# A list scheduler that models the memory port shared by VectorE and GpSimd and picks the engine by it

## The chip, the core and the metric

The kernel runs on one core of one Trainium2 chip. A core has TensorE (PE in the profile; its weight loads are shown apart as PEld), VectorE (DVE), ScalarE (ACT), GpSimd (POOL) and SyncE (SP, which here issues all loads and stores), with the memories SBUF and PSUM beside them. The metric is the time of one execution on the device in microseconds (us); runs are compared by their medians.

## The reference

Two networks of two layers each are applied one after the other to the same tensor of 512 tokens by 1024 features, in float32.

```
for l in 0, 1:                                  # first block
    p = rmsnorm(x) @ w_in                       # latents of q and kv, rotary key, a and gate
    attention of 8 heads over 512 tokens (latents up-projected, softmax, values)
    u = silu(layernorm(dwconv31(a * sigmoid(gate))))          # 31 taps over the tokens
    x = x + concat(attention, u) @ w_o
    z = dwconv3(rmsnorm(x) @ w_up);  x = x + (silu(zg) * zv) @ w_down   # 2816 wide
x = rmsnorm(x)
for l in 0, 1:                                  # second block
    m = state_space_mixer(x) if l == 0 else gated_linear_recurrence(x)
    x = layernorm(ALPHA * x + m)
    x = layernorm(ALPHA * x + relu(x @ w1)**2 @ w2)           # 4096 wide
    x = x + sigmoid(x @ w_gate) * (p[l] @ w_proj)
```

## The kernel before

The activations lie feature-major: eight tiles of 128 features by 512 tokens hold x for the whole run. Every product runs in float32r on operands that are split exactly into a high part and a low part, and takes three products (high with high, high with low, low with high) for each 128 x 128 block of a weight matrix (`mm3`, `dense`). The weights are not preloaded: SP loads them unit by unit, 512 KB each as a rule, into three buffers "r". For each unit `weights` (L662) makes the parts: a cast `hi` (by `copy`, L659, on ScalarE or VectorE) and a subtraction `lo = src - hi` (`R.either`, on GpSimd or VectorE), both 128 x 512. Activations are split in the same way by `split_from`.

The stages are, in order: mixer 0 (attention and convolution, `mixer1`, L856), feed-forward 0 (`ffn1`, L1049), mixer 1, feed-forward 1, the state space mixer (`ssd`, L1110), the first squared-relu feed-forward (`mlp`, L1461), the embedding gate (`ple`), the gated recurrence (`hgrn`, L1294), the second `mlp` and `ple`. In a mixer `conv_tile` (L956) runs once for every two heads: 17 of the 31 taps are a chain of multiply-adds on VectorE (an input tile "u" in SBUF, the running sum in SBUF); the other 14 are scaled on ScalarE and added by `R.either` operations. The softmax of a head works on its four query blocks, each with a minimum on VectorE, an exponential on ScalarE, a reciprocal, a scaling, four transposes on TensorE, a copy and a subtraction. `hgrn` treats its eight heads one after the other: a tree of decays built of many half-width operations on VectorE and GpSimd (`R.other`, `R.either`), then short products.

Nothing of this is issued as it is written. The program is recorded: `R.tensor`, `R.vector` and so on make an `Op` with its cost in a model of the core (`cost`, L340; `cost_tensor`, L366), the operations it depends on, and its tiles. An `R.either` operation may run on GpSimd (first choice) or VectorE, an `R.other` operation on VectorE (first choice) or GpSimd (L322); `any` (L380) gives an operation in several forms, the first of them the first choice, as `copy` does with ScalarE before VectorE. The model's costs in ns, for n columns: VectorE 69 + 1.041 n (copies and scalar operations without PSUM 69 + 0.52 n), plus 60 for each per-partition scalar; GpSimd 147 + 2.105 n; ScalarE 93 + 0.833 n, or 51 + 0.833 n where PSUM takes part; a product 2.5 + n / 2.4.

`schedule` (L441) then plays the core. At each step it asks every engine for its best ready operation by the key (earliest start, priority, place in the program), where the earliest start is the latest of the engine's own free time, the ends of the operations before it with a latency for each pair of engines (`LAT`, L323), and buffers; and it takes the best over the engines. The priority is place in the program, less 0.015 of the remaining path, plus 150 for a change of the activation table and plus `second` = 2000 when the engine is not the operation's first choice. An engine that isn't the first choice may take an operation only if it ends no later than the first choice would, plus `eager` = 500 ns. An operation that needs a new buffer must leave some for older operations that still wait for theirs: `KEEP` (L591), two of the eight PSUM banks among them. Operations up to 2400 places behind the oldest open one take part. The result is a fixed order for each engine; on the chip every queue is worked in this order, and semaphores enforce the dependences. All instructions are issued in `issue` and so bear its line (L572) in the profile.

The groups of the profile name tiles by class: "s" is SBUF of up to 2 KB to a partition, "r" raw weights, "u" padded convolution inputs, "t" and "n" small tiles, "V" and "C" vectors and constants.

Of the kernel before, what the change touches and what calls it, by code (L numbers as in the profile page):

```python
# [38 lines left out]
# ---------------------------------------------------------------- weight units  # L39
def weight_units():  # L40
    """(name, layer, first row, row tiles, column pieces); a piece is (start, stop) or (None, zeros)."""
    u = []
# [99 lines left out]
# ---------------------------------------------------------------- small vectors  # L142
def vec_layout():
    """name -> (first column, columns)"""
    o, n = {}, 0

    def add(name, k):
        nonlocal n
        o[name] = (n, k)
        n += k  # L150
    for l in range(DEPTH):
        for name, k in (("g_mix", 8), ("g_q", 3), ("g_kv", 2), ("w_dw_conv", 124), ("b_dw_conv", 4), ("g_conv_ln", 4),
                        ("b_conv_ln", 4), ("g_ffn", 8), ("w_dw_ffn", 132), ("b_dw_ffn", 44)):
            add(f"{name}{l}", k)
    for name, k in (("g_final", 8), ("cw", 96), ("cb", 24), ("nw", 16), ("dskip", 16), ("dtb", 32), ("alog", 32),
                    ("lb", 8), ("hnw", 1), ("ln_g", 32), ("ln_b", 32), ("rope", 6)):
        add(name, k)
    return o, n
# [50 lines left out]
def constants():  # L209
    """[128, *] of 0 and 1: identity, s<=l, all ones, rope sum, two-way selector, level masks"""  # L210
    i = np.arange(P)
    eye = (i[:, None] == i[None, :])
    tri = (i[:, None] <= i[None, :])
    add = np.zeros((P, P))
    for m in range(P):
        add[m % 32::32, m] = 1
    sel = np.zeros((P, 32))
    for k in range(64):
        sel[k, k % 32] = 1
    j, t = i[:, None], i[None, :]  # L220
    mk = []
    for h in LEVELS:
        mk.append((j // (2 * h) == t // (2 * h)) & (j % (2 * h) < h) & (t % (2 * h) >= h))
    return np.ascontiguousarray(np.concatenate([eye, tri, np.ones((P, P)), add, sel] + mk, axis=1).astype(np.float32))
# [5 lines left out]
# ---------------------------------------------------------------- recorded program and its schedule  # L230
class Tl:
    """A tile of the recorded program; its memory is chosen when the program is scheduled."""
# [11 lines left out]
class Ap:  # L244
    """An access pattern on a recorded tile: the steps to rebuild it and the elements it covers."""
# [68 lines left out]
class Op:  # L314
    __slots__ = ("i", "eng", "calls", "cost", "preds", "succs", "npred", "ready", "tiles", "start", "end", "prio", "label", "tab", "tail", "bias", "alts", "done")


class Recorder:
    """Takes the instructions in program order, orders them per engine by a simulation of the core, and issues them."""
# [8 lines left out]
    def __init__(self):  # L328
        self.ops, self.bias, self.label, self.switch = [], 0, "", 150
        self.greed, self.order_w, self.second, self.eager = 0.015, 1.0, 2000, 500  # L330
# [34 lines left out]

    def cost_tensor(self, calls):  # L366
        """A product streams its columns while the weights of the next one load."""
        stream, load = [], []
        for meth, args, kw in calls:
            n, m = args[0].n, args[1].n  # L370
            once = meth == "transpose" or args[1].tl.dt == F32R
            stream += [2.5 + n / 2.4] if once and meth != "transpose" else [2.5 + n / 1.2] * (1 if once else 2)
            load += [107 * m / 128] * (1 if once else 2)
        return sum(max(a, b) for a, b in zip(stream, load[1:] + [107]))

    def together(self, calls):
        """Products of the tensor engine that stay in one run."""
        self.add("tensor", "matmul", (), {}, [("matmul", a, k) for a, k in calls])

    def any(self, *forms):  # L380
        """One operation in several forms (engine, method, arguments, options); the schedule picks one."""
        eng, meth, args, kw = forms[0]
        self.add(eng, meth, args, kw)
        self.ops[-1].alts = [(e, self.cost(e, m, a, k), [(m, a, k)]) for e, m, a, k in forms]

    def add(self, eng, meth, args, kw, calls=None):
        o = Op()
        calls = calls or [(meth, args, kw)]
        if eng == "tensor":
            o.alts = [(eng, self.cost_tensor(calls), calls)]  # L390
        else:
            o.alts = [(e, self.cost(e, meth, args, kw), calls) for e in self.EITHER.get(eng, (eng,))]
        eng = o.alts[0][0]
# [47 lines left out]
    def schedule(self, slots, keep, window=2400):  # L441
        """Order all operations. slots: class -> buffers; keep: class -> buffers that an operation
        leaves for older operations that still have to take theirs."""
# [28 lines left out]
        table, loads = None, 0  # L472
        while n < len(ops):
# [3 lines left out]
            for p in self.PARTS:  # L477
                t0 = busy[p]
                cand = None
                for o in ready[p]:  # L480
# [5 lines left out]
                    s = max(t0, s)  # L486
# [26 lines left out]
                    if not ok:  # L513
                        continue
                    key = (s, o.prio + (self.switch if load else 0) + (self.second if p != o.alts[0][0] else 0), o.i)
# [6 lines left out]
            (s, _, _), o, p = best  # L522
            o.start = s
            o.eng, o.cost, o.calls = [x for x in o.alts if x[0] == p][0]
# [3 lines left out]
            if o.eng == "sync":  # L528
                size = o.tiles[0].shape[0] * int(np.prod(o.tiles[0].shape[1:])) * 4
                busy["sync"] = s + max(60, size / 330.0)  # L530
                o.end = s + 2000 + size / 330.0
            else:
                o.end = s + o.cost
                if o.tab and table not in o.tab:
                    table = o.tab[0]
                    o.end += 1283
                    loads += 1
                busy[o.eng] = o.end
            n += 1
# [35 lines left out]
# activation tables: function -> the sets that hold it; a set stays loaded while it serves  # L575
# [13 lines left out]
# ---------------------------------------------------------------- the program  # L589
SLOTS = {"psum": 8, "r": 3, "s": 86, "u": 4, "t": 12, "n": 24, "V": 1, "C": 1}  # L590
KEEP = {"psum": 2, "s": 18, "u": 2, "t": 6, "n": 16}  # L591
# [7 lines left out]
def record(R, xT, pos, wts, vecs, consts, pT, outT, dbg=None, stop=None):  # L599
# [37 lines left out]
    def stacked(name, l):  # L637
        """The next unit, of at most 64 columns, with its two float32r parts side by side."""
# [23 lines left out]
    def weights(name, l=None):  # L662
        """The next unit: loaded, and split exactly into two float32r parts."""
# [25 lines left out]
    # ------------------------------------------------ helpers  # L689
# [56 lines left out]
    def gained(name):  # L746
        """x * g as an operand; the row factor is applied to the products"""
        op = []
# [45 lines left out]
    def project(name, l, a, cuts=FULL, scale=None, then=None):  # L794
        """x += a @ w for the row tiles in a, over units of 256 columns"""
# [12 lines left out]
    def products(name, l, n, op, use, cuts=FULL, cols=P):  # L808
        """use(i, slice, product) for n units against op"""
# [9 lines left out]
    # ------------------------------------------------ rope tables  # L819
# [35 lines left out]
    # ------------------------------------------------ block 1: attention and convolution mixer  # L855
    def mixer1(l):  # L856
# [55 lines left out]
        # shared rotary key, four copies down the partitions  # L912
# [16 lines left out]
        # row factors of the latents on all partitions  # L929
# [7 lines left out]
        # values, token-major  # L937
# [39 lines left out]
        for h in range(HEADS):  # L977
# [45 lines left out]
            # the parts of v lie in the two halves of the rows  # L1023
# [12 lines left out]
        # norm and gate of the convolution branch  # L1036
# [11 lines left out]
    # ------------------------------------------------ block 1: gated feed-forward  # L1048
# [60 lines left out]
    # ------------------------------------------------ block 2, layer 0: state space mixer  # L1109
    def ssd(op):  # L1110
# [3 lines left out]
        # step sizes, token-major  # L1114
# [13 lines left out]
        # log(1 + e) = 2 atanh(e / (2 + e)), e = exp(-|x|)  # L1128
# [164 lines left out]
    # ------------------------------------------------ block 2, layer 1: gated linear recurrence mixer  # L1293
    def hgrn(op):  # L1294
# [11 lines left out]
        # lower bound: softmax over the layers, running sum, less the first  # L1306
# [10 lines left out]
        for h in range(8):  # L1317
            # log forget gate and input gate
# [32 lines left out]
            # running sums of the log gates over 64 tokens, then the decay tree below them  # L1351
# [30 lines left out]
            # over a whole chunk: decay from its start and to its end  # L1382
# [9 lines left out]
            # scores [s, l] of the four chunks  # L1392
# [19 lines left out]
            # states between the chunks  # L1412
# [19 lines left out]
            # normed by token, then back to features  # L1432
# [27 lines left out]
    # ------------------------------------------------ block 2: squared relu feed-forward  # L1460
# [24 lines left out]
    # ------------------------------------------------ block 2: per-layer embedding gate  # L1485
    embedded = {}

    def embed(l, half):
        """Half of p @ w_proj. It waits for nothing else: it can stand where the tensor engine would idle."""
# [50 lines left out]
    # ------------------------------------------------ the two blocks  # L1540
    R.label = "start"
    # products of zeros while the first loads run: they open the clock gate of the tensor engine
# [88 lines left out]
```

## Time and profile before

| | |
|---|---|
| time of the runs | 2942.33, 2937.53, 2938.12 us; median 2938.12 |
| the profiled execution: span from the first to the last instruction | 2940.1 us; its own time is not listed apart, and the span stands for it |
| instructions | 37496 |
| mean granted TensorE clock | 0.977 |
| DMA | 235.26 MB, mean 80 GB/s |
| GpSimd's instructions | 1163 |
| VectorE's instructions | 2962 |
| ScalarE's instructions | 2162 |

A group of instructions is shown as: line, engine, operation, what it writes <- what it reads (by class of tile), shapes, x count | busy us, mean ns of one | idle time of the engine just before them, and what ended it. The duration of one instruction counts from where the engine begins on it, so that a wait inside the instruction (for a memory port, say) shows as a longer instruction and not as idle time. Busy time is the union of the instructions; consecutive ones overlap a little in the records, so sums of durations come out somewhat above it.

### The profile page before, as it was taken

The page shows a single profiled execution, that of the slowest core. Times are in us where ns is not written, and L with a number is a line of the kernel's source. Part 1 is how long each engine was busy: PE and PEld are TensorE (multiplying, and loading weights), DVE is VectorE, ACT ScalarE, POOL GpSimd, SP SyncE. Part 2 cuts the span into 40 slices and gives each one's busy share as a digit, 9 for nine tenths or more (in the row PEclk, how much of TensorE's full clock was granted, in tenths as well). Part 3 has the DMA queues.
Part 4 walks back from the last instruction along what each step waited for, and adds up shares of the span by engine and source line. Part 5 has one row for each costly group of instructions (what it writes and reads, how often), then busy time and mean ns, then how long its engine had stood idle before and what let it go on. Part 6 is the DMA issues. An engine that isn't in the chain of part 4 may idle for free. (4 is left out here: it accounts for less than half of the span.)

```text
span 2940.1 us, 37496 instructions
## 1 busy us (share of the span) xinstructions
PE 2778.7 (95%) x14054; PEld 2283.6 (78%) x14054; DVE 2051.8 (70%) x2962; ACT 1193.5 (41%) x2162; POOL 1459.2 (50%) x1163
## 2 busy tenths in 40 slices
PE   7788999999788999999999999999989999899999
PEld 5566788888577888887667888888878788788888
DVE  8999777766998766675674665455687777745546
ACT  4585332335584332244553333122345563322223
POOL 5786434454875334462254563344564544434443
PEclk8899999999899999999999999999999999999999
DMA  4003213331013223331112422233231113223230
GB/s 161 13 24 122 72 65 108 115 126 35 9 58 115 72 100 94 102 108 37 37 44 79 124 70 95 92 106 109 64 94 44 51 51 99 75 93 108 94 108 30
DMA packets 69445, 235.26 MB, mean 80 GB/s; under 512 B 7824, under 2 KB 11024, under 8 KB 69264
## 3 DMA queue, kind: packets, MB, share of 16 engines
q1 hardware_dynamic: 69264, 232.87, 24.7%
q8 instruction: 111, 1.82, 0.2%
q14 instruction: 70, 0.57, 0.1%
HBM read 230.74 MB, written 2.10 MB: 79 GB/s over the span
## 5 line engine op out<-in xcount | busy, mean ns | idle before, releaser
L572 PE MATMUL psum<-s,s 128*128 128x512 f32 (+2 forms) x12752 | 2709.8, 370 | 73.1 <-DVE s L572 49.7
L572 PEld LDWEIGHTS psum<-s,s 128*128 128x128 f32 (+1 forms) x12752 | 2167.4, 190 | 521.8 <-DVE s L572 62.5
L572 POOL TENSOR_TENSOR s<-r,s 128x512 fp32r<-128x512 f32 (+1 forms) x632 | 894.1, 1434 | 903.6 <-ACT s L572 452.0
L572 POOL TENSOR_TENSOR s<-s,s 128x512 f32<-128x512 f32 (+4 forms) x395 | 468.3, 1201 | 379.0 <-DVE s L572 215.5
L572 ACT CAST s<-r 128x512 fp32r<-128x512 f32 (+1 forms) x681 | 385.4, 609 | 381.8 <-DMA r<-wts 340.1
L572 DVE TENSOR_TENSOR s<-s,s 128x512 fp32r<-128x512 f32 (+4 forms) x453 | 418.3, 935 | 84.9 <-ACT s L572 70.1
L572 DVE TENSOR_TENSOR s<-s,psum 128x512 f32<-128x512 f32 (+2 forms) x400 | 224.6, 590 | 284.0 <-PE psum L572 283.2
L572 DVE SCALAR_TENSOR_TENSOR s<-u,V,s 128x512 f32<-128x512 f32 x304 | 324.1, 1076 | 52.5 <-ACT s L572 49.1
L572 ACT ACTIVATE s<-s 128x512 f32<-128x512 f32 (+1 forms) x338 | 188.8, 578 | 281.5 <-DVE s L572 279.5
L572 ACT ACTIVATE s<-psum 128x512 f32<-128x512 f32 (+2 forms) x174 | 91.5, 527 | 453.3 <-PE psum L572 449.1
L572 ACT ACTIVATE s<-u,V 128x512 f32<-128x512 f32 x200 | 144.3, 760 | 258.2 <-DVE u L572 257.8
L572 DVE TENSOR_TENSOR s<-r,s 128x512 fp32r<-128x512 f32 (+1 forms) x237 | 235.7, 1010 | 12.9 <-ACT s L572 9.3
L572 PE MATMUL psum<-C,s 128*128 128x128 f32 (+1 forms) x500 | 93.2, 282 | 53.2 <-POOL s L572 26.4
L572 DVE SCALAR_TENSOR_TENSOR s<-psum,s 128x512 f32<-128x512 f32 (+1 forms) x88 | 55.7, 638 | 112.1 <-ACT s L572 112.1
L572 DVE CAST s<-r 128x512 fp32r<-128x512 f32 (+1 forms) x188 | 101.3, 554 | 42.3 <-DMA r<-wts 42.2
L572 PEld LDWEIGHTS psum<-C,s 128*128 128x128 f32 x500 | 66.3, 157 | 73.0 <-POOL s L572 27.9
L572 DVE CAST s<-s 128x512 fp32r<-128x512 f32 (+1 forms) x105 | 105.8, 1008 | 8.1 <-POOL s L572 2.9
L572 DVE TENSOR_TENSOR u<-psum,s 128x512 f32<-128x512 f32 x88 | 60.5, 687 | 71.1 <-PE psum L572 70.7
L572 ACT CAST s<-s 128x512 fp32r<-128x512 f32 (+2 forms) x110 | 63.4, 587 | 99.8 <-DVE s L572 86.8
L572 ACT ACT_TABLE_LOAD x70 | 89.8, 1283 | 17.7 <-DVE s L572 14.2
L572 DVE SCALAR_TENSOR_TENSOR s<-psum,V,s 128x511 f32<-128x511 f32 (+4 forms) x90 | 66.4, 745 | 38.7 <-ACT s L572 32.9
L572 DVE TENSOR_TENSOR s<-psum,s 128x512 fp32r<-128x512 f32 (+3 forms) x131 | 84.8, 678 | 3.8 <-PE psum L572 2.1
(85 smaller groups left out, 1052.7 us busy)
## 6 DMA issues: line engine op xcount, KB each, us to landing
r<-wts SPq DMA_DIRECT2D x415, 512.0 KB, 3.6
r<-wts SPq DMA_DIRECT2D x12, 256.0 KB, 2.7
r<-wts SPq DMA_DIRECT2D x8, 384.0 KB, 3.0
s<-xT SPq DMA_DIRECT2D x8, 256.0 KB, 5.8
s<-pT SPq DMA_DIRECT2D x8, 256.0 KB, 4.0
outT<-s SPq DMA_DIRECT2D x16, 128.0 KB, 1.7
r<-wts SPq DMA_DIRECT2D x9, 128.0 KB, 2.1
V<-vecs SPq DMA_DIRECT2D x1, 480.5 KB, 6.7
```

Of the source, the lines that this page charges most:

```text
L572: getattr(eng, meth)(*[res(a) for a in args], **{k: res(v) for k, v in kw.items()})
```

## The change

The scheduler's model and its rules are changed; the recorded program, its operations and their forms stay.

- `shares` says of an operation on an engine whether it uses the shared port: on GpSimd always; on VectorE when it has more than one input of more than one column outside PSUM, and for `tensor_scalar` and `tensor_copy` when the input and the output both lie outside PSUM.
- `schedule` keeps a time `port`, the end of the last operation that uses the port. An operation that shares it can't start before that time, so two of them never overlap in the plan.
- `drag`: in the key, the start of an operation on an engine is set back by half of what it costs there above its cheapest engine. The plan itself uses the true start.
- `second` goes from 2000 to 0 and `eager` from 500 to 0.
- A product of n columns costs 2.5 + n / 2.28 ns in the model instead of 2.5 + n / 2.4.
- `KEEP` holds four PSUM banks for older operations instead of two.

Comments and docstrings are removed too; those lines are left out here.

```diff
@@ class Op
-    __slots__ = ("i", "eng", "calls", "cost", "preds", "succs", "npred", "ready", "tiles", "start", "end", "prio", "label", "tab", "tail", "bias", "alts", "done")
+    __slots__ = ("i", "eng", "calls", "cost", "preds", "succs", "npred", "ready", "tiles", "start", "end", "prio", "label", "tab", "tail", "bias", "alts", "done", "shared")
@@ class Recorder
-        self.greed, self.order_w, self.second, self.eager = 0.015, 1.0, 2000, 500
+        self.greed, self.order_w, self.second, self.eager, self.drag = 0.015, 1.0, 0, 0, 0.5
...
+    @staticmethod
+    def shares(eng, meth, args, kw):
+
+        if eng != "vector":
+            return eng == "gpsimd"
+        out = kw["out"] if "out" in kw else args[0]
+        ins = list(args if "out" in kw else args[1:]) + [v for n, v in kw.items() if n not in ("out", "accum_out")]
+        near = sum(isinstance(a, Ap) and a.n > 1 and a.tl.cls != "psum" for a in ins)
+        if meth in ("tensor_scalar", "tensor_copy"):
+            return near == 1 and out.tl.cls != "psum"
+        return near > 1
+
...
-            stream += [2.5 + n / 2.4] if once and meth != "transpose" else [2.5 + n / 1.2] * (1 if once else 2)
+            stream += [2.5 + n / 2.28] if once and meth != "transpose" else [2.5 + n / 1.2] * (1 if once else 2)
...
     def any(self, *forms):
...
+        self.ops[-1].shared = {e: self.shares(e, m, a, k) for e, m, a, k in forms}
...
     def add(self, eng, meth, args, kw, calls=None):
...
+        o.shared = {e: eng != "tensor" and self.shares(e, meth, args, kw) for e, _, _ in o.alts}
...
     def schedule(self, slots, keep, window=2400):
...
-        table, loads = None, 0
+        table, loads, port = None, 0, 0.0
...
-                    s = max(t0, s)
+                    s = max(t0, s, port) if o.shared[p] else max(t0, s)
...
                     if not ok:
                         continue
+                    s += self.drag * ([x[1] for x in o.alts if x[0] == p][0] - min(x[1] for x in o.alts))
                     key = (s, o.prio + (self.switch if load else 0) + (self.second if p != o.alts[0][0] else 0), o.i)
...
             (s, _, _), o, p = best
+            o.eng, o.cost, o.calls = [x for x in o.alts if x[0] == p][0]
+            s -= self.drag * (o.cost - min(x[1] for x in o.alts))
             o.start = s
-            o.eng, o.cost, o.calls = [x for x in o.alts if x[0] == p][0]
...
                 busy[o.eng] = o.end
+                if o.shared[p]:
+                    port = o.end
...
-KEEP = {"psum": 2, "s": 18, "u": 2, "t": 6, "n": 16}
+KEEP = {"psum": 4, "s": 18, "u": 2, "t": 6, "n": 16}
```

## The prediction

> **What bounds the kernel now.** I read the page first, then the busy time of each engine by stage, then the groups of instructions of each stage with their shapes kept apart, and last the waits and single stretches of the timeline.
>
> ```profile
> span 2940.1 us, 37496 instructions
> ...
> PE 2778.7 (95%) x14054; PEld 2283.6 (78%) x14054; DVE 2051.8 (70%) x2962; ACT 1193.5 (41%) x2162; POOL 1459.2 (50%) x1163
> ```
>
> TensorE stands idle for 2940.1 - 2778.7 = 161 us. Busy times by stage, from the view that cuts the span at the times I give it (columns: stretch, length, then PE, PEld, DVE, ACT and POOL busy with their instructions, granted clock, DMA share, GB/s). The stages are mixer 0, feed-forward 0, mixer 1, feed-forward 1, the state space mixer and the gated recurrence:
>
> ```profile
> 0.00:300.00 300.00, 236.35 (x1080) 186.16 (x1081) 287.54 (x387) 179.16 (x335) 213.65 (x164) 0.92 0.23 78
> 300.00:690.00 390.00, 387.69 (x1691) 318.14 (x1691) 270.01 (x325) 124.83 (x204) 168.06 (x124) 1.00 0.28 97
> 690.00:980.00 290.00, 254.61 (x1160) 204.44 (x1159) 255.38 (x354) 173.91 (x320) 189.13 (x139) 0.93 0.17 54
> 980.00:1290.00 310.00, 310.00 (x1392) 256.18 (x1391) 213.42 (x269) 95.46 (x159) 131.89 (x92) 1.00 0.32 103
> 1290.00:1690.00 400.00, 389.87 (x1857) 290.97 (x1857) 254.40 (x468) 178.16 (x294) 172.49 (x141) 0.99 0.20 63
> 2060.00:2550.00 490.00, 449.26 (x3157) 396.26 (x3156) 361.27 (x587) 230.18 (x447) 252.90 (x236) 0.97 0.21 67
> ```
>
> Where PE is busy all the time (300 to 690 and 980 to 1290) no order of the other engines can help. The idle time lies in mixer 0 (63.7 us), mixer 1 (35.4) and the recurrence (40.7), 139.8 of the 161; the granted clock is low there too. In mixer 0 VectorE is busy for 96% of the stage. The next rows, groups over the whole span, show what that busy time is made of:
>
> ```profile
> L572 DVE SCALAR_TENSOR_TENSOR s<-u,V,s 128x512 f32<-128x512 f32 x304 | 324.1, 1076 | 52.5 <-ACT s L572 49.1
> ...
> L572 DVE TENSOR_TENSOR s<-psum,s 128x512 fp32r<-128x512 f32 x64 | 41.8, 675 | 0.7 <-ACT s L572 0.6
> ...
> L572 DVE SCALAR_TENSOR_TENSOR s<-s,V,psum 128x512 f32<-128x512 f32 x32 | 22.8, 743 | 15.9 <-PE psum L572 15.0 <-POOL s L572 0.8
> ```
>
> The same multiply-add takes 743 ns with one input in PSUM and 1076 with both in SBUF. So VectorE waits inside its instructions while GpSimd holds something that both need, the port of the change. What the pieces take undisturbed, from two quieter stretches (1862 to 1960 for VectorE, 1372 to 1470 for GpSimd), beside the 675 and 743 above:
>
> ```profile
> L572 DVE CAST s<-r 128x512 fp32r<-128x512 f32 x3 | 1.3, 427 | 5.1 <-DMA r<-wts 5.1
> ```
> ```profile
> L572 POOL TENSOR_TENSOR s<-r,s 128x512 fp32r<-128x512 f32 x8 | 10.2, 1290 | 12.3 <-ACT s L572 11.6 <-DVE s L572 0.8
> L572 POOL TENSOR_TENSOR s<-s,s 128x512 f32<-128x512 f32 x6 | 7.6, 1280 | 32.5 <-ACT s L572 32.5
> ```
>
> **Moving work off the port.** Mixer 0 (0 to 300), VectorE and then GpSimd:
>
> ```profile
> L572 DVE SCALAR_TENSOR_TENSOR s<-u,V,s 128x512 f32<-128x512 f32 x64 | 78.2, 1258 | 0.0
> L572 DVE TENSOR_TENSOR s<-s,s 128x512 f32<-128x512 f32 x18 | 23.2, 1292 | 1.3 <-POOL s L572 1.2
> L572 DVE CAST s<-r 128x512 fp32r<-128x512 f32 x30 | 22.4, 765 | 0.0
> L572 DVE TENSOR_TENSOR s<-psum,s 128x512 fp32r<-128x512 f32 x32 | 20.8, 676 | 0.5 <-ACT s L572 0.5
> L572 DVE TENSOR_REDUCE n<-psum 128x1 f32<-128x512 f32 x32 | 20.8, 674 | 0.0
> L572 DVE TENSOR_TENSOR s<-r,s 128x512 fp32r<-128x512 f32 x22 | 17.8, 815 | 0.4 <-ACT s L572 0.3
> L572 DVE TENSOR_TENSOR s<-s,psum 128x512 f32<-128x512 f32 x24 | 15.5, 678 | 1.9 <-PE psum L572 1.9
> L572 DVE SCALAR_TENSOR_TENSOR s<-s,V,s 128x512 fp32r<-128x512 f32 x14 | 15.2, 1100 | 6.5 <-ACT s L572 6.5
> ```
> ```profile
> L572 POOL TENSOR_TENSOR s<-s,s 128x512 f32<-128x512 f32 x60 | 93.6, 1574 | 21.8 <-ACT s L572 14.9 <-DVE s L572 5.9 <-DVE n L572 0.6
> L572 POOL TENSOR_TENSOR s<-r,s 128x512 fp32r<-128x512 f32 x47 | 71.1, 1530 | 34.2 <-DVE s L572 17.9 <-ACT s L572 10.3 <-PE psum L572 3.5
> L572 POOL TENSOR_TENSOR s<-s,s 128x512 fp32r<-128x512 f32 x11 | 16.4, 1495 | 3.4 <-ACT s L572 1.9 <-DVE s L572 1.1 <-DVE n L572 0.4
> ```
>
> VectorE's stall in these rows: 64 x (1258 - 743) = 33.0 us, 18 x (1292 - 675) = 11.1, 30 x (765 - 427) = 10.1, 22 x (815 - 675) = 3.1, 14 x (1100 - 743) = 5.0; together 62 of its 287.5, so 225 us are its own work. GpSimd's stall: 60 x (1574 - 1280) + 47 x (1530 - 1290) + 11 x (1495 - 1285) = 31, so 182 of its 213.7 are its own. The port is held for those 182 and for VectorE's two-input work and casts at undisturbed pace: 64 x 0.743 + (18 + 22) x 0.675 + 30 x 0.427 + 14 x 0.743 = 98. That is 280 of 300 us, smaller groups left out: the port is nearly full.
>
> The new rule moves work. An operation that either engine may do (the second engine's handicap of 2000 points and its allowance of 500 ns are both gone) costs the port 1.285 us on GpSimd and 0.675 on VectorE. With x operations moved to VectorE the port needs 280 - 0.61x and VectorE 225 + 0.675x; the two meet at x = 43 and 254 us, so the best is 300 - 254 = 46 us. By the code all but some two of these 118 GpSimd operations are free to move. The drag decides how many do: for GpSimd it adds half of 1225 - 602 (the scheduler's own costs for 512 columns), 311 ns, so GpSimd gets one only while VectorE is committed for longer than that beyond the release of the port, in practice during a PSUM operation. Those are the three PSUM rows, 32 + 32 + 24 = 88. The 73 operations left on GpSimd then have 88 / 73 = 1.2 of them each, 0.81 us of cover for 1.285 us; VectorE's two-input work stands for 0.47 x 73 = 34 us. Gain 46 - 34 = 12; with one PSUM operation to each it is 46 - 0.61 x 73 = 1.5. I take 12, between ends of 1.5 and 46.
>
> Mixer 1 (690 to 980):
>
> ```profile
> L572 DVE SCALAR_TENSOR_TENSOR s<-u,V,s 128x512 f32<-128x512 f32 x80 | 87.8, 1107 | 6.0 <-ACT s L572 5.4
> L572 DVE TENSOR_TENSOR s<-s,s 128x512 f32<-128x512 f32 x21 | 27.2, 1296 | 0.2
> ...
> L572 DVE TENSOR_TENSOR s<-r,s 128x512 fp32r<-128x512 f32 x17 | 17.5, 1042 | 0.9 <-ACT s L572 0.9
> ```
> ```profile
> L572 POOL TENSOR_TENSOR s<-s,s 128x512 f32<-128x512 f32 x54 | 81.5, 1524 | 21.4 <-ACT s L572 13.7 <-DVE s L572 7.0
> L572 POOL TENSOR_TENSOR s<-r,s 128x512 fp32r<-128x512 f32 x38 | 57.4, 1523 | 41.2 <-DVE s L572 19.1 <-ACT s L572 15.6 <-issue 4.7
> ```
>
> In the same way VectorE stalls for 29.1 + 13.0 + 6.2 = 48 us and has 207 of its own, GpSimd stalls for 22 and has 167, the port is held for 167 + 85 = 252. They meet at x = 35 and 231 us: at best 59 us less. With one PSUM operation to each of the 56 left, 59 - 34 = 25. But TensorE is idle for only 35.4 us of this stage, and each head's chain (minimum, exponential, reciprocal, transposes) keeps part of that. I take half of the idle time, 18; ends 0 and 59.
>
> **The gated recurrence** (2060 to 2550). No engine is full; heads follow each other as chains. VectorE's rows there, and the shares of the chain that ended last between 2350 and 2450:
>
> ```profile
> L572 DVE TENSOR_TENSOR s<-s,s 128x256 f32<-128x256 f32 x77 | 48.8, 656 | 2.0 <-POOL s L572 1.5
> L572 DVE TENSOR_TENSOR s<-s 128x256 f32<-128x256 f32 x64 | 48.8, 811 | 0.0
> L572 DVE TENSOR_TENSOR s<-r,s 128x512 fp32r<-128x512 f32 x40 | 41.3, 1043 | 1.9 <-ACT s L572 1.5
> ...
> L572 DVE TENSOR_TENSOR s<-s,psum 128x256 f32<-128x256 f32 x48 | 17.2, 413 | 9.2 <-PE psum L572 9.1
> ```
> ```profile
> by line: DVE s L572 47.5%; PE psum L572 31.9%; issue 5.9%; DMA r<-wts 5.2%; ACT s L572 4.3%; ACT L572 3.8%; POOL s L572 2.7%; POOL n L572 1.4%; DVE n L572 0.1%; POOLq L572 0.0%; ACTq L572 0.0%
> ```
>
> Against 413 ns for half a row and 675 for a whole one, the stall is 18.7 + 25.5 + 14.7 = 59 us. If 47.5% of it lies on the chain, 28 us could go. I take two thirds, 18, since weight splits moved to VectorE queue ahead of chain steps; ends 0 and the 40.7 us of idle TensorE.
>
> **What the port rule overstates.** Two rows of the timeline:
>
> ```profile
> 934.27 1.28 DVE L572 TENSOR_TENSOR s<-r,s 128x512 fp32r<-128x512 f32 x2
> ```
> ```profile
> 934.44 1.49 POOL L572 TENSOR_TENSOR n<-n,n 128x4 f32<-128x4 f32 x1 [2.88 <-DVE n L572]
> ```
>
> Two VectorE operations with two SBUF inputs run at 0.64 us each inside a GpSimd power. The change holds its port for the power's whole modelled time and so plans a hole of about 1 us on VectorE beside each. A planned hole does not exist on the chip, where a queue simply goes on, so I cost it at nothing; should the order put chain work behind it, it costs 1.49 us each; a mixer has four by the code, 6 us.
>
> The Trainium skill ("SBUF — State Buffer", Who interferes with whom) says that a two-input VectorE instruction and a GpSimd instruction that reads SBUF exclude each other for the whole instruction. The wide rows agree (1258 against 743 ns); the power beside two operations of 0.64 us does not. By that rule the planned hole is one that the chip has anyway, and the 48 us below stay whole; by the rows it is needless, and up to 6 us in each mixer are lost of them.
>
> **Edits at nothing.** The product pace changes plan only: 2.5 + 512/2.28 = 227 ns instead of 216. In feed-forward 1 the 310 us hold 1392 products, 223 ns each with the short ones in, so the new figure is the nearer. Where PE is full this changes nothing; elsewhere its worth lies inside the terms above, and its cost if the order turns out worse is the third rival's. KEEP at 4 instead of 2 holds PSUM banks back for older work; it adds no instruction, and its price is that rival too. No DMA is added; SP issues the same loads in an order that follows the new plan.
>
> **Sum.** 12 + 18 + 18 = 48 us off the profiled span of 2940.1, which lies 2.0 above the median of 2938.1: 2892 on the span, 2890 on the median. A difference of 0.2%, 6 us, is about what a measurement of this kernel can tell from no change.
>
> **The rivals.** First, *nothing comes of it*: the moved work fills just what the stalls leave, 62 us in mixer 0 against 92 x 0.675. For it: the one-PSUM-operation end of 1.5 us, and costs of 602 and 1225 ns that the change leaves below the 675 and 1285 of the rows, so plan and chip drift apart. 2938; chance 0.10. Second, *VectorE becomes the bound* (slower): the drag sends it nearly everything, casts too, since it also adds 92 ns to a cast on ScalarE (half of 520 - 335 by the scheduler's costs). In mixer 0 it decides from x = (300 - 225) / 0.675 = 111 of the 116. With all of them and as many casts again as the 30 of the row, 225 + 78 + 13 = 316, 16 us over; mixer 1, with 207 + 62 + 13 = 282 of 290, stays as it is, and the recurrence wins nothing: 2954. Against it: ScalarE, busy for 179 of 300, takes a cast whenever VectorE is later than those 92 ns. Chance 0.08. Third, *KEEP stops TensorE from running ahead* (slower): a later product needs a bank beyond four kept, so at most three are filled ahead of order; it decides where the chain of a head outlasts three banks of 24 products, 3 x 24 x 0.223 = 16 us. If that costs each of the eight heads one bank's work, 5.4 us, the recurrence loses 43 instead of winning 18, and with the mixers' 30 kept 2938 + 43 - 30 = 2951; without them 2981. Chance 0.12. Fourth, *the balance is met*: 46 + 35 + 28 = 109 us, 2829; chance 0.15, because the exact lock is now planned instead of met by accident.
>
> **How the numbers follow.** The forecast (some 10 to 80 us gained) has 0.55. Faster: 0.55 + 0.15 = 0.70; same 0.10; slower 0.08 + 0.12 = 0.20. The range of 2825 to 2965 takes in the balance at its low end and the milder slow cases at its high end; the likeliest case by itself spans 2858 to 2928.
>
> **What would show it.** Right: fewer GpSimd instructions than 1163, VectorE's multiply-adds on u near 0.8 to 0.9 us instead of 1.08, mixers shorter, the feed-forward stages unchanged. Wrong: VectorE idle-free and PE idle longer in the mixers (second rival), PE idle longer in the recurrence behind ScalarE and VectorE with their rows short (third), or instruction counts moved and stages of the same length (first).

## The result and the profile after

The changed kernel takes 2852.15 us (median of four runs) against 2939.79 us of the kernel before on the same chip: a ratio of 0.970, 95% interval 0.9686 to 0.9714, 88 us less where 48 were forecast. The profiled execution ran 2849.06 us with a span of 2846.7. All comparisons leave out two executions in a slower state, one of 7111.52 us of the kernel before and one of 4023.39 us in a run with two passes, so that the medians of these two groups are 2937.15 and 2894.58 us. The page of the changed kernel, whose instructions bear line 590 now:

```profile
span 2846.7 us, 37062 instructions
...
PE 2753.9 (97%) x14054; PEld 2269.8 (80%) x14054; DVE 1969.7 (69%) x3426; ACT 1215.5 (43%) x2202; POOL 795.0 (28%) x657
...
L590 DVE SCALAR_TENSOR_TENSOR s<-u,V,s 128x512 f32<-128x512 f32 x304 | 260.0, 859 | 49.7 <-ACT s L590 47.5
```

GpSimd has 657 instructions instead of 1163, VectorE 3426 instead of 2962, and yet VectorE is busy for 82 us less: its multiply-adds take 859 ns instead of 1076. TensorE's idle time falls from 161.4 to 92.8 us, by 69, and its busy time by 25.

For the stages both kernels are cut at the same points of the work, where GpSimd takes the power of the norms between them (the products in a stretch agree within twenty). Busy times by stage of the kernel before, then of the changed one, with the columns as in the prediction; the rows are mixer 0, feed-forward 0, mixer 1, feed-forward 1, the state space mixer and the recurrence:

```profile
0.00:306.00 306.00, 240.04 (x1097) 188.93 (x1098) 292.22 (x394) 182.00 (x339) 214.92 (x166) 0.92 0.23 79
306.00:698.00 392.00, 392.00 (x1714) 322.09 (x1713) 265.33 (x318) 121.99 (x199) 166.79 (x123) 1.00 0.28 95
698.00:934.00 236.00, 200.61 (x924) 160.06 (x924) 224.83 (x314) 156.30 (x294) 171.36 (x126) 0.92 0.16 52
934.00:1295.00 361.00, 359.37 (x1614) 296.97 (x1613) 248.59 (x318) 117.20 (x194) 153.18 (x108) 1.00 0.31 97
1295.00:1737.00 442.00, 431.55 (x2120) 328.42 (x2119) 277.07 (x509) 187.58 (x311) 198.01 (x164) 0.99 0.21 66
2104.00:2493.00 389.00, 358.93 (x2568) 312.86 (x2567) 295.98 (x466) 200.09 (x381) 201.91 (x187) 0.97 0.21 64
```
```profile
0.00:280.00 280.00, 241.46 (x1097) 192.62 (x1098) 263.33 (x458) 185.46 (x344) 106.05 (x93) 0.93 0.25 84
280.00:674.00 394.00, 394.00 (x1716) 320.94 (x1715) 253.85 (x378) 128.13 (x210) 66.56 (x56) 1.00 0.28 96
674.00:901.00 227.00, 197.28 (x923) 157.92 (x923) 215.19 (x358) 162.02 (x303) 103.51 (x76) 0.95 0.17 52
901.00:1259.00 358.00, 358.00 (x1595) 293.16 (x1594) 241.30 (x369) 120.60 (x198) 59.58 (x43) 1.00 0.31 101
1259.00:1686.00 427.00, 420.97 (x2119) 323.40 (x2118) 285.69 (x556) 187.76 (x315) 128.83 (x109) 1.00 0.21 66
2054.00:2406.00 352.00, 346.39 (x2562) 307.97 (x2561) 270.86 (x557) 208.61 (x398) 96.39 (x82) 1.00 0.23 73
```

Mixer 0 is 26 us shorter, mixer 1 9, the state space mixer 15, the recurrence 37; the feed-forward stages, where TensorE was full, change by 2 and 3. The six stages together are 88 us shorter, the two profiled spans 93. In mixer 0 VectorE does 64 more instructions in 29 us less. Its groups there, and GpSimd's, in the changed kernel:

```profile
L590 DVE SCALAR_TENSOR_TENSOR s<-u,V,s 128x512 f32<-128x512 f32 x64 | 56.6, 888 | 0.0
L590 DVE TENSOR_TENSOR s<-r,s 128x512 fp32r<-128x512 f32 x54 | 36.0, 697 | 0.6 <-ACT s L590 0.5
L590 DVE TENSOR_TENSOR s<-s,s 128x512 f32<-128x512 f32 x42 | 32.7, 785 | 0.1
```
```profile
L590 POOL TENSOR_TENSOR s<-s,s 128x512 f32<-128x512 f32 x39 | 57.4, 1481 | 54.7 <-DVE s L590 45.7 <-ACT s L590 8.5
L590 POOL TENSOR_TENSOR s<-r,s 128x512 fp32r<-128x512 f32 x14 | 22.2, 1598 | 25.2 <-DVE s L590 18.6 <-ACT s L590 6.6
...
L590 POOL TENSOR_TENSOR s<-s,s 128x512 fp32r<-128x512 f32 x4 | 5.2, 1291 | 4.1 <-ACT s L590 4.1
```

Of the 118 wide operations on GpSimd 57 are left, so about 61 moved, against 43 for the balance of the prediction. The same three groups of VectorE stalled for 33 + 11 + 3 = 47 us before; now 64 x (888 - 743) + 42 x (785 - 675) + 54 x (697 - 675) = 15 us. GpSimd stands idle in front of its operations, waiting for VectorE's results.

In the recurrence the shares of the chain that ended last, before (2104 to 2493) and after (2054 to 2406), say it in one line each:

```profile
by line: PE psum L572 40.3%; DVE s L572 31.9%; issue 4.5%; DMA r<-wts 2.8%; ACT s L572 1.9%; ACT L572 1.3%; POOL s L572 1.3%; POOL n L572 0.4%; DVE n L572 0.2%; DVEq L572 0.0%; POOLq L572 0.0%; ACTq L572 0.0%; SPq L572 0.0%
```
```profile
by line: PE psum L590 92.4%; DVE s L590 5.0%; DMA r<-wts 1.4%; ACT s L590 0.5%; issue 0.5%; POOL s L590 0.2%; POOLq L590 0.0%; DVEq L590 0.0%; SPq L590 0.0%
```

The chain of the kernel before is known only from 2168 us on, so its shares add up to 85%. It was one of VectorE and TensorE in turn; now it is TensorE almost alone, which is idle for 5.6 us instead of 30.1 there. The groups of VectorE behind that, before and after, in the same two stretches:

```profile
L572 DVE TENSOR_TENSOR s<-s 128x256 f32<-128x256 f32 x64 | 48.8, 811 | 0.0
L572 DVE TENSOR_TENSOR s<-s,s 128x256 f32<-128x256 f32 x63 | 39.5, 652 | 1.1 <-POOL s L572 0.9
L572 DVE TENSOR_TENSOR s<-r,s 128x512 fp32r<-128x512 f32 x33 | 33.8, 1036 | 1.9 <-ACT s L572 1.5
```
```profile
L590 DVE TENSOR_TENSOR s<-r,s 128x512 fp32r<-128x512 f32 x70 | 48.6, 713 | 2.0 <-ACT s L590 1.8
L590 DVE TENSOR_TENSOR s<-s,s 128x256 f32<-128x256 f32 x96 | 45.3, 503 | 1.1 <-POOL s L590 0.9
L590 DVE TENSOR_TENSOR s<-s 128x256 f32<-128x256 f32 x67 | 27.7, 457 | 0.0
```

Against 675 ns for a whole row and 413 for half a one, the three stalled for 12 + 15 + 25 = 52 us before and for 3 + 9 + 3 = 15 us after.

### The profile page after: what moved, and what is told of

It is laid out like the page before. It is cut to its first block, busy times and chain, and to the rows that moved or that the text cites. A ratio compares the mean times of both kernels' runs of the same rounds, so it can differ in the third digit from the quotient of the medians.

```text
span 2846.7 us, 37062 instructions
## 1 busy us (share of the span) xinstructions
PE 2753.9 (97%) x14054; PEld 2269.8 (80%) x14054; DVE 1969.7 (69%) x3426; ACT 1215.5 (43%) x2202; POOL 795.0 (28%) x657
## 4 chain that ended last, share of the span: by engine, by line
PE 82%; DVE 12%; issue 3%; ACT 2%; DMA 0%; POOL 0%; POOLq 0%; DVEq 0%; ACTq 0%; SPq 0%
PE psum L590 82%; DVE s L590 11%; ACT s L590 2%; DVE n L590 1%; DMA r<-wts 0%; ACT L590 0%; POOL n L590 0%; POOL s L590 0%; DVE u L590 0%; POOL u L590 0%; POOLq L590 0%; DVEq L590 0%; ACTq L590 0%; SPq L590 0%; POOLq L1641 0%
## 5 line engine op out<-in xcount | busy, mean ns | idle before, releaser
L590 PE MATMUL psum<-s,s 128*128 128x512 f32 (+3 forms) x12752 | 2683.4, 368 | 65.8 <-DVE s L590 52.8
L590 POOL TENSOR_TENSOR s<-r,s 128x512 fp32r<-128x512 f32 (+1 forms) x341 | 468.2, 1390 | 1086.2 <-ACT s L590 625.6
L590 ACT CAST s<-r 128x512 fp32r<-128x512 f32 (+1 forms) x704 | 400.9, 610 | 375.4 <-DMA r<-wts 356.9
L590 DVE TENSOR_TENSOR s<-s,s 128x512 fp32r<-128x512 f32 (+6 forms) x641 | 422.4, 678 | 77.4 <-ACT s L590 66.9
L590 POOL TENSOR_TENSOR s<-s,s 128x512 f32<-128x512 f32 (+5 forms) x207 | 254.6, 1240 | 622.7 <-DVE s L590 395.8
L590 DVE TENSOR_TENSOR s<-r,s 128x512 fp32r<-128x512 f32 (+1 forms) x528 | 366.0, 720 | 5.8 <-ACT s L590 3.8
L590 DVE SCALAR_TENSOR_TENSOR s<-u,V,s 128x512 f32<-128x512 f32 x304 | 260.0, 859 | 49.7 <-ACT s L590 47.5
L590 DVE CAST s<-r 128x512 fp32r<-128x512 f32 (+1 forms) x165 | 70.4, 441 | 39.3 <-DMA r<-wts 37.8
L590 POOL TENSOR_TENSOR n<-n,n 128x4 f32<-128x4 f32 (+1 forms) x32 | 34.7, 1083 | 194.8 <-DVE n L590 194.5
```

What stands on the lines that cost most here:

```text
L590: getattr(eng, meth)(*[res(a) for a in args], **{k: res(v) for k, v in kw.items()})
```

## The experiments

Every time stands beside runs of the kernel before on the same chip (2937.15 us for the first four runs, 2940.60 for the three with two passes and the one with everything on VectorE, 2940.97 for the other four). Four theories were told apart. A: the port's time in the plan and the new choice of engine carry the gain together. B: fewer operations on GpSimd are all of it. C: the PSUM reserve and the product pace carry it. Later D and E: who does the work, against when it is done.

**Without the port in the plan.**

```diff
-                    s = max(t0, s, port) if o.shared[p] else max(t0, s)
+                    s = max(t0, s)
```

> The changed kernel with the port taken out of the plan: a shared operation no longer waits for the port's time; engine choice by drag, product pace and PSUM reserve stay. Theory A (the port's plan and the choice both carry the gain): GpSimd keeps its small share, about 650 to 800 instructions, but two-input work of VectorE meets it again, the multiply-adds on u go from 859 ns back towards 950 to 1000, and 20 to 30 us of the 88 come back: about 2875 us. Theory B (fewer operations on GpSimd are the whole gain, the port's time adds nothing): 2852 within 6 us. Theory C (pace and PSUM reserve carry it): 2852 within 6 us too.

Measured 2947.57 us, ratio 1.0034 (1.0021 to 1.0046): not 20 or 30 us but all of the gain is lost. The engines and the multiply-adds of this run:

```profile
PE 2783.3 (95%) x14054; PEld 2287.2 (78%) x14054; DVE 2031.4 (69%) x3058; ACT 1190.8 (40%) x2148; POOL 1365.8 (46%) x1081
...
L590 DVE SCALAR_TENSOR_TENSOR s<-u,V,s 128x512 f32<-128x512 f32 x304 | 312.5, 1034 | 57.0 <-ACT s L590 53.2
```

With the same drag and the same thresholds GpSimd is back at 1081 instructions and the stall is back. Theory A had the direction and neither the size nor the count. Theory C falls here: the reserve and the pace were kept, and the gain is gone. Theory B isn't judged, since GpSimd did not stay with few operations. The drag by itself sends little to VectorE; an engine that the plan holds to be free is used.

**The old choice with the port.**

```diff
-        self.greed, self.order_w, self.second, self.eager, self.drag = 0.015, 1.0, 0, 0, 0.5
+        self.greed, self.order_w, self.second, self.eager, self.drag = 0.015, 1.0, 2000, 500, 0.0
```

> The changed kernel with the old choice of engine: the handicap of 2000, the allowance of 500 ns, no drag; the port's time, pace and reserve stay. Theory A: half of the gain is lost, GpSimd has 900 or more instructions, 2890 to 2905 us. Theory B: nearly all is lost, 2930 to 2940. Theory C: nothing is lost, 2852 within 6.

Measured 2913.19 us, ratio 0.9915 (0.9899 to 0.993): 24 us better than before, 61 worse than the changed kernel.

```profile
PE 2780.5 (95%) x14054; PEld 2278.7 (78%) x14054; DVE 1596.8 (55%) x2439; ACT 1293.9 (44%) x2351; POOL 1822.1 (63%) x1497
...
L590 DVE SCALAR_TENSOR_TENSOR s<-u,V,s 128x512 f32<-128x512 f32 x304 | 321.8, 1071 | 58.9 <-ACT s L590 55.7
```

GpSimd, the first choice of the splits, now has 1497 instructions, more than before the change, and the multiply-adds take 1071 ns, as before it: an order that plans no two users of the port at once does not keep them from meeting on the chip. The 24 us lie within the scatter that a control below shows, so this run is no proof against B. The new choice is needed for the 88 us: with both, the plan keeps 657 instructions on GpSimd.

**Two PSUM banks held back instead of four.**

```diff
-KEEP = {"psum": 4, "s": 18, "u": 2, "t": 6, "n": 16}
+KEEP = {"psum": 2, "s": 18, "u": 2, "t": 6, "n": 16}
```

> The changed kernel with two PSUM banks held back for older work instead of four. Theories A and B: 2852 within 8 us, as the reserve adds no work. Theory C: the recurrence, which won twice of what was forecast, gives back 20 us or more: 2872 or above.

Measured 2852.64 us, ratio 0.9711 (0.9694 to 0.9728).

**The old product pace.**

```diff
-            stream += [2.5 + n / 2.28] if once and meth != "transpose" else [2.5 + n / 1.2] * (1 if once else 2)
+            stream += [2.5 + n / 2.4] if once and meth != "transpose" else [2.5 + n / 1.2] * (1 if once else 2)
```

> The changed kernel with the old product pace of 2.5 + n/2.4 in the plan. Theories A and B: 2852 within 8 us. Theory C: 10 us or more are lost, 2862 or above.

Measured 2856.32 us, ratio 0.9721 (0.9706 to 0.9736). Neither gives back what theory C asked for, 20 and 10 us; whether they matter by less is not to be seen, for a reason that the control further below shows.

**Who and when.** Two passes: the first fixes the engine of each operation, the second plans the order with these engines.

```diff
-    R = Recorder()
-    record(R, xT, pos, wts, vecs, consts, pT, outT, dbg, stop)
+    A, R = Recorder(), Recorder()
+    A.lock = True
+    for r in (A, R):
+        record(r, xT, pos, wts, vecs, consts, pT, outT, dbg, stop)
+    A.schedule(SLOTS, KEEP)
+    for x, o in zip(A.ops, R.ops):
+        o.alts = [f for f in o.alts if f[0] == x.eng]
+        o.eng, o.cost, o.calls = o.alts[0]
+    R.lock = False
     R.schedule(SLOTS, KEEP)
```

`lock` says whether the port's time takes part. The engines of the changed kernel, an order without the port:

> The program is planned twice. The first pass is the changed scheduler and fixes which engine does each operation (657 instructions on GpSimd); the second pass keeps these engines and plans the order anew without the port's time. Theory D (who does the work carries the gain: less on GpSimd means less to wait for): 2852 to 2870 us, VectorE's multiply-adds on u below 900 ns. Theory E (when it is done carries it: two users of the port are never planned at once): most of the gain is lost, 2910 to 2940 us, multiply-adds on u at 1000 ns or more.

Measured 2894.58 us, ratio 0.9847 (0.9831 to 0.9864). Its multiply-adds:

```profile
L591 DVE SCALAR_TENSOR_TENSOR s<-u,V,s 128x512 f32<-128x512 f32 x304 | 264.7, 872 | 49.3 <-ACT s L591 47.0
```

The control, `R.lock = True`:

> The control to the run without the port's time: the same two passes and the same engines, the second pass with the port's time. Both theories: 2852 within 12 us, a little off because the second pass has no choice left to make.

Measured 2875.48 us, ratio 0.978 (0.9765 to 0.9794), 23 us above the changed kernel, with multiply-adds of 831 ns. The other way round, the engines by the old rules without the port and the order with it (`A.lock, A.second, A.eager, A.drag = False, 2000, 500, 0.0`, `R.lock = True`):

> The first pass fixes the engines by the old rules without the port (some 1170 instructions on GpSimd, as before); the second pass plans the order with the port's time. Theory D: 2920 to 2940 us. Theory E: half of the gain or more is there, below 2895 us.

Measured 2892.38 us, ratio 0.9839 (0.9824 to 0.9853). Its engines and multiply-adds:

```profile
PE 2767.4 (96%) x14054; PEld 2270.3 (79%) x14054; DVE 1928.4 (67%) x2944; ACT 1191.6 (41%) x2169; POOL 1447.8 (50%) x1174
...
L591 DVE SCALAR_TENSOR_TENSOR s<-u,V,s 128x512 f32<-128x512 f32 x304 | 308.8, 1025 | 45.8 <-ACT s L591 42.8
```

With GpSimd as full as before (1174 instructions) the order alone gives 48 us, and the engines alone, in an order that knows nothing of the port, give 46. Neither D nor E holds by itself: each brings about half of the 88, and together in two passes 65. The length of the multiply-adds goes by who does the work: 872 and 831 ns with 657 instructions on GpSimd, without and with the port in the order, but 1025 with 1174. The order alone thus gains its 48 us with most of this stall still there, so a shorter stall is not all of the gain; how the order brings the rest isn't shown. What the one pass brings beyond, where engine and time are chosen at once, is 23 us and, as the next control shows, within what such a scheduler scatters by.

**A control of the scatter.**

```diff
-        self.greed, self.order_w, self.second, self.eager, self.drag = 0.015, 1.0, 0, 0, 0.5
+        self.greed, self.order_w, self.second, self.eager, self.drag = 0.016, 1.0, 0, 0, 0.5
```

> The changed kernel with the weight of the remaining path in the priority at 0.016 instead of 0.015. It touches nothing that any theory speaks of; it shows how far the time moves when the list scheduler merely falls another way. 2852 within 10 us; what it moves by is the bound under which no other difference counts.

Measured 2879.14 us, ratio 0.9789 (0.9776 to 0.9803): 27 us worse by an edit that means nothing (the first value, the weight of the remaining path in the priority); the 10 us expected were too narrow a bound. GpSimd has 652 instructions against 657, the multiply-adds take 850 ns against 859; in the main only the order fell another way. So one schedule against another says nothing below some 27 us, and this bound rests on a single such edit; the true one may be larger. The 46, 48, 61, 65 and 95 us above lie beyond it; the 24 us of the old choice with the port, the 23 us of the control, the 19 us between the two orders with the new engines, and the results of the reserve and the pace don't, and none of the four runs below differs from the changed kernel by more.

**Everything on VectorE.**

```diff
-    EITHER = {"either": ("gpsimd", "vector"), "other": ("vector", "gpsimd")}
+    EITHER = {"either": ("vector",), "other": ("vector",)}
```

> The changed kernel with every operation of free choice on VectorE: some 114 instructions are left on GpSimd. Theory D taken alone would have the gain grow: below 2852. The second rival of the prediction (VectorE becomes the bound in mixer 0 from 111 moved operations on): mixer 0 gets 10 to 20 us longer than in the changed kernel, the recurrence longer too, 2870 to 2900 in all.

Measured 2853.24 us, ratio 0.9705 (0.9689 to 0.9722): the time of the changed kernel, with a GpSimd that is busy for 3% of the span.

```profile
PE 2754.6 (97%) x14054; PEld 2272.3 (80%) x14054; DVE 2074.4 (73%) x3950; ACT 1227.6 (43%) x2219; POOL 79.5 (3%) x114
...
L590 DVE SCALAR_TENSOR_TENSOR s<-u,V,s 128x512 f32<-128x512 f32 x304 | 226.5, 745 | 34.6 <-ACT s L590 32.6
```

Here the multiply-add takes 745 ns, the undisturbed figure. Theory D taken alone would have had the gain grow; it did not. Mixer 0, up to the same power, takes 287 us against 280, the recurrence 343 against 352 (with 2536 products against 2562, so that a part of these 9 us is a difference of the cut):

```profile
0.00:287.00 287.00, 243.70 (x1100) 191.37 (x1101) 275.54 (x515) 187.59 (x340) 13.66 (x31) 0.90 0.22 75
2049.00:2392.00 343.00, 341.76 (x2536) 304.23 (x2535) 276.59 (x621) 206.48 (x392) 21.66 (x24) 1.00 0.23 69
```

**Powers and memsets not counted as users of the port.**

```diff
-            return eng == "gpsimd"
+            return eng == "gpsimd" and kw.get("op") != ALU.pow and meth != "memset"
```

> The changed kernel with GpSimd's powers and memsets no longer counted as users of the port in the plan. The prediction held that the planned holes beside powers cost nothing on the chip, 6 us in each mixer at most: 2840 to 2855 us if that holds, nothing that exceeds the control with another path weight. If the whole-instruction rule held for powers, VectorE's two-input work beside them would now stall and the time would grow by some 10 us.

Measured 2865.45 us, ratio 0.9744 (0.9731 to 0.9757): 13 us worse, within the scatter. Whether holes beside powers cost anything stays open.

**No drag.**

```diff
-        self.greed, self.order_w, self.second, self.eager, self.drag = 0.015, 1.0, 0, 0, 0.5
+        self.greed, self.order_w, self.second, self.eager, self.drag = 0.015, 1.0, 0, 0, 0.0
```

> The changed kernel with a drag of 0. If the drag decides how many operations leave GpSimd, as the prediction said, GpSimd's 657 instructions go back towards 1000 and 20 us or more are lost: 2872 or above. If the port's time itself sends them to VectorE, because a 602 ns operation lets the next one in sooner than one of 1225, the count stays near 700 and the time within 10 us of 2852.

Measured 2866.00 us, ratio 0.9745 (0.9731 to 0.9758), with 725 instructions on GpSimd against 657. The 14 us are within the scatter, but the count seems to be more than that: with another reserve, pace or path weight, or with powers outside the port, it stayed between 651 and 664. The drag moves some 68 operations; the rest go by the port's time and the loss of the handicap together, as neither is enough by itself (1081 without the port's time, 1497 with the old choice).

**A mixed version.**

```diff
+        self.solo = False
...
-            o.alts = [(e, self.cost(e, meth, args, kw), calls) for e in self.EITHER.get(eng, (eng,))]
+            o.alts = [(e, self.cost(e, meth, args, kw), calls) for e in (("vector",) if self.solo and eng in self.EITHER else self.EITHER.get(eng, (eng,)))]
...
     for l in range(DEPTH):
+        R.solo = l == 1
         fill(f"mix{l}")
```

> The changed kernel with every operation of free choice on VectorE in the second block's second layer (recurrence, feed-forward, gate) and the free choice elsewhere. By the stages of the run with everything on VectorE, the recurrence and what follows were 10 and 9 us shorter there, the first mixer and the state space mixer 6 and 10 us longer: the sum of the better stages is 19 us below the changed kernel, about 2833. If the stages do not add up, 2852.

Measured 2839.28 us, ratio 0.9653 (0.964 to 0.9666), against 0.970 (0.9686 to 0.9714) for the changed kernel. As a kernel it is the fastest of all that ran, 13 us below the changed one where 19 were expected. As evidence for its idea the 13 us are within the scatter.

## Why the prediction was right, point by point

**The size.** The 88 us lie outside the 10 to 80 that the likeliest case allowed, and nearer to the 109 of the fourth rival than to 48. The stated range holds the result because it takes in that rival. The direction and the mechanism were right; of the four stages that gained, two were put too low, one too high, and one at nothing. Part of the 88 may also be luck of one order: the changed kernel, its versions with another reserve, pace, path weight, drag or count of powers, the control with two passes, the mixed version and the one with everything on VectorE took 2839 to 2879 us, and it is the second fastest of these nine.

**The bound.** Right: VectorE and GpSimd waited for each other inside their instructions, and most of the gain came where TensorE had idle time, the feed-forward stages keeping their lengths (392 and 394, 361 and 358 us). That the two engines' meeting is the cause does not rest on the traces alone: it takes the run without the port in the plan, where the stall and the time are back, and the run with everything on VectorE, where the stall is gone and the gain is whole. How the gain divides between fewer meetings and a better order is open.

**Mixer 0**, 12 us forecast, 26 measured, inside the ends of 1.5 and 46. The terms were mis-sized. More operations moved than 43 (61). VectorE's own work was put at 225 us; with nearly all on VectorE and no one to wait for, it had 515 - 394 = 121 instructions more than before in this stage and was busy for 275.5 us, and at 0.60 us each the 121 are 73, so its own work is some 203, an estimate that takes all 121 for full width. The stall of before was then nearer to 89 of 292 us than to 62; the five groups summed left the smaller ones out. In the changed kernel 64 more instructions add 38 us to the 203, which leaves some 22 of the 263 us for the stall: VectorE lost some 67 us of stall and took on 38 of work, 29 net, and the stage followed with 26. And 0.60 us it is, not 0.675, as the timeline of the changed kernel shows:

```profile
152.40 1.12 DVE L590 SCALAR_TENSOR_TENSOR s<-u,V,s 128x512 f32<-128x512 f32 x1
153.44 0.68 DVE L590 TENSOR_TENSOR s<-r,s 128x512 fp32r<-128x512 f32 x1
154.04 0.74 DVE L590 SCALAR_TENSOR_TENSOR s<-u,V,s 128x512 f32<-128x512 f32 x1
```

An operation of 0.68 us lets the next begin after 0.60: durations of neighbours overlap in the records. The scheduler's 602 ns, which the first rival called too short, is the pace from start to start.

**Mixer 1**, 18 forecast, 9 measured, inside 0 and 59: its ends were too wide to be of use, and half of the idle time, 18 us, was a guess. Of the 35.4 us TensorE is still idle for 29.7 there.

**The recurrence**, 18 forecast, 37 measured, inside the 40.7 us of idle time that were taken as its end. The step that failed is the worth of a stall: three groups' 59 us times the chain's share, and then two thirds of it for moved splits that would queue ahead of chain steps. The splits did not hold up the chain, in which VectorE has 5.0% after, and the stall of the three groups went for the most part (52 us to 15). TensorE lost 24.5 us of idle time, near the 28 before the cut to two thirds, and 12.5 us of busy time, the granted clock going from 0.97 to 1.00; the busy time was no term of the prediction. That the 28 were near is in part luck: their 47.5% came from one stretch of 100 us, and over the whole stage VectorE had 31.9%.

**The state space mixer**, 0 forecast, 15 measured. The prediction measured the recoverable time by idle time alone (10.1 us there). Of the 15 us, 4.4 were idle time and 10.6 busy time of TensorE, for the same 2120 products. A busy TensorE was not one at its pace.

**The drag** was named as what decides how many operations leave GpSimd. That step failed: without it 725 remain, without the port's time 1081. By the code, an operation that both engines may do and that waits for the port can start on either at the same time, the port's. With the handicap gone such a tie goes to VectorE, which `schedule` asks first, so GpSimd gets the operation only while VectorE is busy beyond the port's release. That is what the prediction put down to the drag alone.

**The hole beside a power.** Open. The run without powers and memsets in the port cannot tell 6 us in a mixer from the scatter. The reading behind it is weaker than it was put: of the two operations the first began at 934.27, before the power at 934.44, so only the second began beside it.

**The edits at nothing.** The pace and the reserve moved the time by 4 and 0.5 us: as forecast, within scatter.

**The rivals.** Nothing of it: refuted. VectorE as the bound: with all operations there mixer 0 took 287 us, 19 less than before the change, where 316 were priced: 22 us too many of VectorE's own work, 116 x 0.075 = 9 too many for the moved operations. Within the scatter it is as fast as the changed kernel. The reserve: refuted at its price of 43 us in the recurrence, which won 37; with two banks the time is 2852.64 us. The balance met (109 us gained): nearest of the rivals; the recurrence exceeded its part (37 against 28), the mixers stayed below theirs (26 and 9 against 46 and 35).

## What to carry to other kernels

If two engines share a port, a plan that does not know of it sees free time where there is none, and a rule for the choice of engine that rests on this plan chooses wrongly: here the rule without the port was worth nothing, and both together 88 us. Before attributing anything to one edit of a scheduler, change something that means nothing and see how far the time goes; here it went 27 us, further than seven of the other eleven edits moved the changed kernel. Ask also what the simplest plan would do: with all free work on VectorE the port is left with almost nothing to order, and the time was the same. Whether the scheduler of before would be as fast with that one edit wasn't run. Work out an engine's load from starts to starts, not from sums of durations, and look for lost time of TensorE in its busy time too.

## What was not expected of the hardware

VectorE alone could do all the elementwise work that was free to move (GpSimd busy for 79.5 us instead of 795.0) at the same total time, each wide operation moved took it 0.60 us from start to start in the timeline above and took one of 1.28 to 1.29 us off the port. Durations of neighbouring VectorE instructions overlap by about 0.08 us in the records (1.12 us long, the next begun after 1.04; 0.68 and 0.60).
